# Retention scores of two heads alternating on two halves of the rows, output products grouped by array shape

## The chip, the cores and the metric

The kernel runs on one core of one Trainium2 chip. The core has five engines with queues of their own: TensorE (PE, matrix products), VectorE (DVE), ScalarE (ACT), GpSimd (POOL) and SyncE (SP, which issues most transfers). The metric is the time of one execution on the device in microseconds, the median of several runs.

## The reference

Two layers work on a sequence of 16 meta tokens and 512 tokens with 1024 channels. In each layer a projection feeds three mixers side by side: six heads of stick-breaking attention, six heads of retention (64 channels each), and a state-space mixer (S5). Their outputs are concatenated, projected back, and followed by a gated MLP. The change touches retention alone, which works by chunks of 128 positions:

```python
scores = jnp.einsum('bhnid,bhnjd->bhnij', qc, kc) * decay_in[None, :, None]
inner = jnp.einsum('bhnij,bhnje->bhnie', scores, vc.astype(jnp.float32))
...
cross = jnp.einsum('bhid,bhde->bhie', qn, state)
state = state * chunk_decay[None, :, None, None] + jnp.einsum('bhjd,bhje->bhde', kn, vn)
...
o = inner + jnp.moveaxis(cross, 0, 2)
```

So within a chunk the output is the masked scores times the values, and what came before the chunk enters through the state. The kernel has the decay folded into tables by which q and k are multiplied, so that a plain triangular mask is left. Its five chunks are the first 512 positions in four of 128, and a last one of 16.

## The kernel before

Activations lie with channels on the 128 partitions and the 528 positions along the free dimension. Two heads of 64 channels share a tile: head 0 has partitions 0 to 63, head 1 the rest. The large products (projections, output projection, MLP) are made in three parts of reduced fp32 each, recorded as `pj` with the operands `xh`, `xl` or `hi`, `lo` (activations) and `wh`, `wl` (weights). They are emitted by `mm3`, which after each k step calls `tick`.

The mixers are generators ("lanes") that are resumed by `tick` between the products of a projection, so their instructions are woven into TensorE's queue between `pj` products. What is resumed when is decided by a planner: `spend` (line 96) keeps a clock for each engine, `mm` (line 128) charges a product's estimated time to TensorE's clock, and a lane goes on when its last step's estimated end is at most 200 ns ahead of TensorE's clock. A lane that needs PSUM banks takes credits (`banks`, five in all) and gives them back (`freed`). A scheduler of the framework then orders the emitted instructions once more by its own simulation of readiness. On the chip each engine works through its queue in order and waits on semaphores.

`ret_pair` (line 931) is the lane of one pair of heads; three pairs per layer run one after another, six in all. It transposes v and k (`rtp`), makes the chunk states (`kv`, summed into `st`), and then, from line 968: for each head in turn four score products of 128x128 into one bank `ps` and one of 16x16 into a second bank `ps2` (both recorded as `sc`), with 64 rows of the array each; two DVE operations multiply them by the mask `keep` into an SBUF tile `sc`. Then (line 986) for each chunk the two heads' outputs `ro` from `sc` and `rv`, 64 columns of the array each, and for all chunks but the first a product of the full array that adds the state's part (`ro` from `rm` and `st`). ACT copies the result out (`o`), and a head norm (`hps`), a gate and a split follow. All products of `ret_pair` are fp32; the trace holds two records for each, one for each pass.

The attention lanes (`sb_group`, line 815) make `z` from `sq` and `sk` with 64 rows of the array too; the two heads run as two lanes.

Of the kernel before, what the change touches and what calls it, by code (L numbers as in the profile page):

```python
# [8 lines left out]
F32 = mybir.dt.float32  # L9
# [3 lines left out]
ALU = mybir.AluOpType  # L13
PSUM = bass.MemoryType.PSUM

P = 128
NM = 16
# [33 lines left out]
def width(g):  # L51
    return g[-1][3] + g[-1][2] - g[-1][1]
# [36 lines left out]
def hybrid_kernel(ctx, tc, A, out, dbg=None):  # L89
# [6 lines left out]
    def spend(key, ns):  # L96
        t = now[0]
        start = max(busy[key], busy["PE"])
        if t:
            if key != t[3]:  # L100
                t[3], t[4] = key, t[1]
            start = max(start, t[4])
            t[1] = max(t[1], start + ns + HOP)
        busy[key] = start + ns
# [19 lines left out]
    V = Timed(nc.vector, "V", 70, 1.05)  # L124
# [3 lines left out]
    def mm(out, lhsT, rhs, start, stop, more=False):  # L128

        n = out.shape[-1] / 2.4  # L130
        spend("PE", 2 * max(107.0, 2 * n) if rhs.dtype == F32 else max(107.0, n) + 3)
        nc.tensor.matmul(out, lhsT=lhsT, rhs=rhs, start=start, stop=stop, skip_group_check=more)  # L132

    class TE:
# [18 lines left out]
    def nm(s):  # L153
        uid[0] += 1
        return f"{s}_{uid[0]}"

    def tt(s="t"):
        return tp.tile([P, T], F32, tag="t", name=nm(s))

    def bank(s="b"):  # L160
        return mx.tile([P, 512], F32, tag="mx", name=nm(s))
# [10 lines left out]
    def take(what, n):  # L172

        if free[what] < n:
            yield lambda: free[what] >= n
        free[what] -= n

    def banks(n):
        yield from take("bank", n)

    def freed(n, what="bank"):
        free[what] += n
# [34 lines left out]
    def const(shape, dt, name):  # L217
        return cp.tile(shape, dt, tag=name, name=name)
# [9 lines left out]
    for name, g in (("A", G_A), ("B2", G_B2)):  # L228
        n = width(g)
        m = masks[n] = const([P, n], BF16, "mask" + name)  # L230
        G.memset(m, 0.0)
        for j, q0, q1, o0 in g:
            c = slice(o0, o0 + min(q1 - q0, P))
# [6 lines left out]
    keep = const([P, P], F32, "keep")  # L240
# [98 lines left out]
    def open_ps(nt, s="pj"):  # L339
        return [bank(s), bank(s)] if nt == T else [bank(s)]  # L340
# [82 lines left out]
    def headnorm(t, gcol):  # L423

        s = tt("hsq")
        SC.activation(s, t, AF.Square)
        yield
        yield from banks(2)
        pss = []
        for i in range(2):  # L430
            ps = bank("hps")
            mm(ps[:, :HALF], lhsT=blk, rhs=s[:, HALF * i:HALF * i + HALF], start=True, stop=True)
            pss.append(ps)
        yield
        for i, ps in enumerate(pss):
            rs_from(ps[:, :HALF], s, HALF * i, HALF)
        rs_exp(s)
        yield
        freed(2)
        V.scalar_tensor_tensor(out=t, in0=t, scalar=cols[:, gcol:gcol + 1], in1=s, op0=ALU.mult, op1=ALU.mult)  # L440
        yield
# [489 lines left out]
    def ret_pair(l, p, q, k, vt, gate, res):  # L931
        v = gp.tile([P, 640], F32, tag="g", name=nm("rv"))
        kt = tt("kt")
        for src, dst in ((vt, v), (k, kt)):
            yield from banks(1)
            ps = bank("rtp")
            for j in range(4):
                TE.transpose(ps[:, P * j:P * j + P], src[:, P * j:P * j + P], ident)
            yield
            SC.copy(out=dst[:, :512], in_=ps)  # L940
            yield
            freed(1)
        yield from banks(1)
        ps = bank("rtp")
        TE.transpose(ps[:NM, :P], vt[:, 512:528], ident)
        yield
        SC.copy(out=v[:NM, 512:640], in_=ps[:NM, :P])
        yield
        freed(1)

        st = tt("st")
        G.memset(st, 0.0)
        yield from banks(1)
        ps = bank("kv")
        for j in range(4):
            mm(ps[:, P * j:P * j + P], lhsT=kt[:, P * j:P * j + P], rhs=v[:, P * j:P * j + P], start=True, stop=True)
        yield
        for hh in range(2):
            r, c = slice(64 * hh, 64 * hh + 64), 64 * hh
            SC.copy(out=st[r, c:c + 64], in_=ps[r, c:c + 64])  # L960
        yield
        for j in range(1, 4):
            for hh in range(2):
                r, c = slice(64 * hh, 64 * hh + 64), P * j + 64 * hh
                V.tensor_tensor(out=st[r, c:c + 64], in0=st[r, c - P:c - P + 64], in1=ps[r, c:c + 64], op=ALU.add)
        yield
        freed(1)
        scs = []
        for hh in range(2):
            r = slice(64 * hh, 64 * hh + 64)  # L970
            sc = tt("sc")
            yield from banks(2)
            ps, ps2 = bank("sc"), bank("sc")
            for j in range(4):
                mm(ps[:, P * j:P * j + P], lhsT=k[r, P * j:P * j + P], rhs=q[r, P * j:P * j + P], start=True, stop=True)
            mm(ps2[:NM, :NM], lhsT=k[r, 512:528], rhs=q[r, 512:528], start=True, stop=True)
            yield
            V.tensor_tensor(out=sc[:, :512].rearrange("p (j c) -> p j c", c=P), in0=ps.rearrange("p (j c) -> p j c", c=P),
                            in1=keep[:, None, :].to_broadcast([P, 4, P]), op=ALU.mult)
            V.tensor_tensor(out=sc[:NM, 512:528], in0=ps2[:NM, :NM], in1=keep[:NM, :NM], op=ALU.mult)  # L980
            scs.append(sc)
            yield
            freed(2)
        yield from banks(2)
        op, op2 = bank("ro"), bank("ro")
        for j in range(5):
            n = P if j < 4 else NM
            d = op[:, P * j:P * j + n] if j < 4 else op2[:, :n]
            for hh in range(2):
                r = slice(64 * hh, 64 * hh + 64)  # L990
                mm(d[r], lhsT=v[:n, P * j + 64 * hh:P * j + 64 * hh + 64], rhs=scs[hh][:n, P * j:P * j + n],
                   start=True, stop=j == 0)
            if j:
                mm(d, lhsT=st[:, P * (j - 1):P * j], rhs=q[:, P * j:P * j + n], start=False, stop=True)
            if j == 2:
                yield
        o = tt("o")
        SC.copy(out=o[:, :512], in_=op)
        SC.copy(out=o[:, 512:528], in_=op2[:, :NM])
        yield  # L1000
        freed(2)
        yield from headnorm(o, 80 + 3 * l + p)
        yield lambda: gate() is not None
        rg = gate()
        s = tt("sg")
        V.tensor_scalar(out=s, in0=rg, scalar1=-40.0, scalar2=None, op0=ALU.max)
        yield
        sigmoid(s, s, 1.0)
        yield
        G.tensor_tensor(out=s, in0=s, in1=rg, op=ALU.mult)  # L1010
        yield
        V.tensor_tensor(out=o, in0=o, in1=s, op=ALU.mult)
        dump(f"ro{l}{p}", o)
        yield
        res.append(o)
# [38 lines left out]
    for l in range(LAYERS):  # L1054
# [76 lines left out]
        for ks in OUT_PARTS[l]:  # L1131
            drain(lambda: all(mix[k] is not None for k in ks))
            for m in range(KD):
# [3 lines left out]
                ps = open_ps(nt)  # L1137
# [13 lines left out]
        for n, (kind, i, f0, nf) in enumerate(mlp_order()):  # L1151
            w = weight()
            ps = open_ps(nt)
# [119 lines left out]
```

## Time and profile before

| | us |
|---|---|
| median of three runs | 1395.85 |
| lowest and highest run | 1392.8, 1401.91 |
| profiled execution | 1399.35 |
| its span, first to last instruction | 1397.6 |
| TensorE busy in it | 1370.0 |
| DVE, ACT, POOL busy in it | 807.1, 618.9, 509.2 |

The profile shows one execution. A row of the timeline view is a merged run of like instructions of one engine: its start, its length, the engine, line and operation, the tiles (output, then inputs), the shape (rows*columns of the array that a product uses, then the operands), and how many records it merges; a bracket gives the engine's idle time before it and who ended that. Matmuls overlap, so a length includes the tail of the last one, and the distance between starts is what a stretch costs. In the list of groups three durations are the least, the middle and the greatest in ns.

### The profile page before, as it was taken

To read this page: it belongs to the slowest core of one execution; us is meant where nothing else is said; L and a number is where in the kernel's file an instruction comes from. 1 tells how busy PE (TensorE), PEld (TensorE's weight loads), DVE (VectorE), ACT (ScalarE), POOL (GpSimd) and SP (SyncE) were. 2 spreads that over 40 slices of the span, in tenths; PEclk is the share of its full clock that TensorE was granted. 3 is DMA by queue.
4 is the path that set the end of the run, shared out by engine and by line. 5 is a ranking of instruction groups with operands and counts; after the bars stand their busy time and mean duration, and the time that the engine had idled before them with its cause. 6 is when DMAs were issued, how large, how long until landed. Compare 5 with 4: busy or idle time off the path is not lost.

```text
span 1397.6 us, 22767 instructions
## 1 busy us (share of the span) xinstructions
PE 1370.0 (98%) x9188; PEld 1254.3 (90%) x9188; DVE 807.1 (58%) x1312; ACT 618.9 (44%) x1002; POOL 509.2 (36%) x624
## 2 busy tenths in 40 slices
PE   6999999999999999999999999999999999999998
PEld 6989898999999999999999999998788888888886
DVE  8875557767455545544566477464585543553453
ACT  5456565545343223322354564874363432442231
POOL 5685536322689302200233544362122210220020
PEclk9999799999999999999999999999999999999999
DMA  4212102313221322222222121122232322223223
GB/s 154 69 65 96 38 21 84 97 46 115 97 76 61 106 91 91 90 93 87 80 91 91 61 93 46 56 68 82 79 106 96 100 92 94 101 91 104 93 77 105
DMA packets 38985, 118.27 MB, mean 85 GB/s; under 512 B 4960, under 2 KB 5472, under 8 KB 38880
## 3 DMA queue, kind: packets, MB, share of 16 engines
q1 hardware_dynamic: 38880, 116.82, 25.8%
q8 instruction: 72, 1.18, 0.3%
q14 instruction: 33, 0.27, 0.1%
HBM read 111.46 MB, written 2.10 MB: 81 GB/s over the span
## 4 chain that ended last, share of the span: by engine, by line
PE 85%; DVE 8%; POOL 4%; issue 1%; DMA 1%; ACT 1%; SPq 0%; DVEq 0%; POOLq 0%; ACTq 0%
PE pj L132 71%; PE z L132 6%; PE hps L132 1%; PE ro L132 1%; PE av L132 1%; DVE s5w L121 1%; PE sc L132 1%; PE yps L132 1%; DVE wl L121 1%; POOL lo L121 1%; PE kps L132 1%; DVE sq L121 1%; DVE gg L121 1%; DVE fr L121 0%; PE kv L132 0%
## 5 line engine op out<-in xcount | busy, mean ns | idle before, releaser
L132 PE MATMUL pj<-xh,wh 128*128 128x264 f32 (+1 forms) x1792 | 451.5, 311 | 13.7 <-ACT wh L121 5.2
L132 PE MATMUL pj<-xh,wl 128*128 128x264 f32 (+1 forms) x1792 | 451.6, 311 | 1.6 <-DVE wl L121 1.6
L132 PE MATMUL pj<-xl,wh 128*128 128x264 f32 (+1 forms) x1792 | 449.7, 310 | 1.7 <-DVE xl L121 1.7
L121 ACT CAST wh<-wr 128x1024 fp32r<-128x1024 f32 (+3 forms) x209 | 206.0, 987 | 417.5 <-PE pj L132 381.8
L132 PEld LDWEIGHTS pj<-xh,wh 128*128 128x128 f32 x1792 | 298.3, 191 | 31.3 <-issue 7.5
L132 PEld LDWEIGHTS pj<-xl,wh 128*128 128x128 f32 x1792 | 298.5, 190 | 19.6 <-DVE xl L121 2.4
L132 PEld LDWEIGHTS pj<-xh,wl 128*128 128x128 f32 x1792 | 298.2, 190 | 19.3 <-issue 2.0
L121 DVE TENSOR_TENSOR wl<-wr,wh 128x1024 fp32r<-128x1024 f32 (+3 forms) x166 | 249.2, 1502 | 73.7 <-ACT wh L121 71.3
L132 PE MATMUL pj<-hi,wh 128*128 128x264 f32 (+1 forms) x720 | 192.9, 323 | 0.0
L132 PE MATMUL pj<-lo,wh 128*128 128x264 f32 (+1 forms) x720 | 192.3, 321 | 0.0
L132 PE MATMUL pj<-hi,wl 128*128 128x264 f32 (+1 forms) x720 | 191.7, 321 | 0.1
L121 POOL TENSOR_TENSOR up<-ga,up 128x528 f32<-128x528 f32 (+1 forms) x44 | 61.8, 1405 | 345.6 <-DVE up L121 345.6
L121 DVE TENSOR_TENSOR h<-h,pj 128x264 f32<-128x264 f32 (+1 forms) x144 | 69.2, 511 | 135.1 <-PE pj L132 135.0
L121 POOL TENSOR_TENSOR wl<-wr,wh 128x1024 fp32r<-128x1024 f32 (+2 forms) x43 | 95.6, 2223 | 130.4 <-ACT wh L121 122.9
L132 PEld LDWEIGHTS pj<-hi,wh 128*128 128x128 f32 x720 | 119.4, 188 | 11.0 <-ACT wh L121 0.6
L132 PEld LDWEIGHTS pj<-hi,wl 128*128 128x128 f32 x720 | 119.4, 188 | 10.9 <-DVE wl L121 0.5
L132 PEld LDWEIGHTS pj<-lo,wh 128*128 128x128 f32 x720 | 119.4, 188 | 10.3
L121 POOL TENSOR_TENSOR lo<-ga,hi 128x528 fp32r<-128x528 f32 (+1 forms) x44 | 58.9, 1339 | 158.7 <-ACT hi L121 158.6
L121 DVE TENSOR_TENSOR up<-pj,R 128x264 f32<-128x264 f32 (+1 forms) x66 | 32.2, 515 | 95.2 <-PE pj L132 95.2
L121 ACT ACTIVATE si<-si,bias 128x528 f32<-128x528 f32 (+1 forms) x44 | 32.1, 731 | 94.3 <-DVE si L121 94.3
L121 DVE TENSOR_TENSOR ga<-si,up 128x528 f32<-128x528 f32 (+1 forms) x44 | 31.7, 720 | 72.7 <-ACT si L121 56.8
L121 ACT ACTIVATE e<-z 128x512 f32<-128x512 f32 (+2 forms) x72 | 39.3, 546 | 63.2 <-PE z L132 57.2
(228 smaller groups left out, 1747.1 us busy)
## 6 DMA issues: line engine op xcount, KB each, us to landing
wr<-in_w_in_dram SPq DMA_DIRECT2D x45, 512.0 KB, 3.5
wr<-in_w_gate_dram SPq DMA_DIRECT2D x44, 512.0 KB, 3.4
wr<-in_w_up_dram SPq DMA_DIRECT2D x44, 512.0 KB, 3.4
wr<-in_w_down_dram SPq DMA_DIRECT2D x32, 512.0 KB, 3.4
wr<-in_w_out_dram SPq DMA_DIRECT2D x16, 384.0 KB, 3.2
wr<-in_w_down_dram SPq DMA_DIRECT2D x16, 384.0 KB, 3.1
rc<-in_rope_dram SPq DMA_DIRECT2D x12, 264.0 KB, 3.7
rs<-in_rope_dram SPq DMA_DIRECT2D x12, 264.0 KB, 4.0
```

What stands on the lines that cost most here:

```text
L121: return f(*a, **k)
L132: nc.tensor.matmul(out, lhsT=lhsT, rhs=rhs, start=start, stop=stop, skip_group_check=more)
```

## The change

Three things change. `mm` charges TensorE's clock only half for each product with a 64 among the partitions of its moving operand or output; this holds for the scores, for the outputs from `sc`, and for `z` from `sq`. In the scores, one bank for each head and a shared one for the two 16x16 products are taken together; the 16x16 product of head 0 comes first, then the 128x128 products alternate between the heads, so between rows 0 to 63 and 64 to 127 of the array; the 16x16 product of head 1 follows once DVE has read that of head 0 from the shared bank. In the outputs, all products from `sc` come first, and those from the state after them.

```diff
@@ -128,7 +128,8 @@
     def mm(out, lhsT, rhs, start, stop, more=False):
 
         n = out.shape[-1] / 2.4
-        spend("PE", 2 * max(107.0, 2 * n) if rhs.dtype == F32 else max(107.0, n) + 3)
+        t = 2 * max(107.0, 2 * n) if rhs.dtype == F32 else max(107.0, n) + 3
+        spend("PE", t / 2 if 64 in (rhs.shape[0], out.shape[0]) else t)
         nc.tensor.matmul(out, lhsT=lhsT, rhs=rhs, start=start, stop=stop, skip_group_check=more)
 
     class TE:
@@ -965,35 +966,43 @@
                 V.tensor_tensor(out=st[r, c:c + 64], in0=st[r, c - P:c - P + 64], in1=ps[r, c:c + 64], op=ALU.add)
         yield
         freed(1)
-        scs = []
-        for hh in range(2):
-            r = slice(64 * hh, 64 * hh + 64)
-            sc = tt("sc")
-            yield from banks(2)
-            ps, ps2 = bank("sc"), bank("sc")
-            for j in range(4):
-                mm(ps[:, P * j:P * j + P], lhsT=k[r, P * j:P * j + P], rhs=q[r, P * j:P * j + P], start=True, stop=True)
-            mm(ps2[:NM, :NM], lhsT=k[r, 512:528], rhs=q[r, 512:528], start=True, stop=True)
-            yield
+
+        scs = [tt("sc"), tt("sc")]
+        yield from banks(3)
+        pss, ps2 = [bank("sc"), bank("sc")], bank("sc")
+
+        def score(hh, j):
+            r, n = slice(64 * hh, 64 * hh + 64), P if j < 4 else NM
+            c = slice(P * j, P * j + n)
+            mm(pss[hh][:, c] if j < 4 else ps2[:n, :n], lhsT=k[r, c], rhs=q[r, c], start=True, stop=True)
+
+        def kept_last(sc):
+            V.tensor_tensor(out=sc[:NM, 512:528], in0=ps2[:NM, :NM], in1=keep[:NM, :NM], op=ALU.mult)
+        score(0, 4)
+        for j in range(4):
+            for hh in range(2):
+                score(hh, j)
+        yield
+        kept_last(scs[0])
+        for sc, ps in zip(scs, pss):
             V.tensor_tensor(out=sc[:, :512].rearrange("p (j c) -> p j c", c=P), in0=ps.rearrange("p (j c) -> p j c", c=P),
                             in1=keep[:, None, :].to_broadcast([P, 4, P]), op=ALU.mult)
-            V.tensor_tensor(out=sc[:NM, 512:528], in0=ps2[:NM, :NM], in1=keep[:NM, :NM], op=ALU.mult)
-            scs.append(sc)
-            yield
-            freed(2)
+        score(1, 4)
+        yield
+        kept_last(scs[1])
+        yield
+        freed(3)
         yield from banks(2)
         op, op2 = bank("ro"), bank("ro")
-        for j in range(5):
-            n = P if j < 4 else NM
-            d = op[:, P * j:P * j + n] if j < 4 else op2[:, :n]
+
+        tiles = [(j, P if j < 4 else NM, op[:, P * j:P * j + P] if j < 4 else op2[:, :NM]) for j in range(5)]
+        for j, n, d in tiles:
             for hh in range(2):
-                r = slice(64 * hh, 64 * hh + 64)
-                mm(d[r], lhsT=v[:n, P * j + 64 * hh:P * j + 64 * hh + 64], rhs=scs[hh][:n, P * j:P * j + n],
-                   start=True, stop=j == 0)
-            if j:
-                mm(d, lhsT=st[:, P * (j - 1):P * j], rhs=q[:, P * j:P * j + n], start=False, stop=True)
-            if j == 2:
-                yield
+                mm(d[64 * hh:64 * hh + 64], lhsT=v[:n, P * j + 64 * hh:P * j + 64 * hh + 64],
+                   rhs=scs[hh][:n, P * j:P * j + n], start=j in (0, 4), stop=True, more=True)
+        yield
+        for j, n, d in tiles[1:]:
+            mm(d, lhsT=st[:, P * (j - 1):P * j], rhs=q[:, P * j:P * j + n], start=False, stop=True, more=True)
         o = tt("o")
         SC.copy(out=o[:, :512], in_=op)
         SC.copy(out=o[:, 512:528], in_=op2[:, :NM])
```

All six pairs change alike; the places below are in the program's last pair (second layer) and in the lanes of the first layer. `order` here means the sequence of instructions in one engine's queue, without times.

TensorE, the scores of the last pair before; `rm` are q and k, `pj` are products of the output projection, and x4 merges four like rows:

```order
L132 MATMUL pj_11476<-hi_10871,wh_11395 128x512
L132 MATMUL sc_11483<-rm_11131,rm_11300 128x128 x4
L132 MATMUL sc_11484<-rm_11131,rm_11300 16x16
L132 MATMUL pj_11476<-lo_10872,wh_11395 128x512
L132 MATMUL pj_11476<-hi_10871,wl_11396 128x512
L132 MATMUL pj_11497<-hi_9633,wh_11430 128x512
L132 MATMUL pj_11497<-lo_9634,wh_11430 128x512
L132 MATMUL pj_11497<-hi_9633,wl_11431 128x512
L132 MATMUL sc_11502<-rm_11131,rm_11300 128x128 x4
L132 MATMUL sc_11503<-rm_11131,rm_11300 16x16
L132 MATMUL pj_11497<-hi_10725,wh_11430 128x512
```

There are two stretches of `sc`, one for each head, with `pj` between them.

The same place after the change, from the third of the four alternations on (ahead of these rows stand `sc_11444` 16x16, then twice `sc_11442` and `sc_11443`):

```order
L133 MATMUL sc_11442<-rm_11113,rm_11256 128x128
L133 MATMUL sc_11443<-rm_11113,rm_11256 128x128
L133 MATMUL sc_11442<-rm_11113,rm_11256 128x128
L133 MATMUL sc_11443<-rm_11113,rm_11256 128x128
L133 MATMUL pj_11438<-lo_10816,wh_11375 128x512
L133 MATMUL pj_11438<-hi_10815,wl_11376 128x512
L133 MATMUL pj_11438<-hi_10910,wh_11375 128x512
L133 MATMUL pj_11438<-lo_10911,wh_11375 128x512
L133 MATMUL pj_11438<-hi_10910,wl_11376 128x512
L133 MATMUL sc_11444<-rm_11113,rm_11256 16x16
```

The heads alternate in one stretch, and the second 16x16 product stands alone, five `pj` later.

TensorE, the outputs of the last pair before, from where head 1 joins:

```order
L132 MATMUL ro_11519<-sc_11501,rv_11409 64x128
L132 MATMUL ro_11519<-sc_11482,rv_11409 64x128
L132 MATMUL ro_11519<-sc_11501,rv_11409 64x128
L132 MATMUL ro_11519<-rm_11131,st_11453 128x128
L132 MATMUL ro_11519<-sc_11482,rv_11409 64x128
L132 MATMUL ro_11519<-sc_11501,rv_11409 64x128
L132 MATMUL ro_11519<-rm_11131,st_11453 128x128
L132 MATMUL ro_11519<-sc_11482,rv_11409 64x128
L132 MATMUL ro_11519<-sc_11501,rv_11409 64x128
L132 MATMUL ro_11519<-rm_11131,st_11453 128x128
L132 MATMUL ro_11520<-sc_11501,rv_11409 64x16
L132 MATMUL ro_11520<-rm_11131,st_11453 128x16
```

Products with 64 output rows and products from the state alternate chunk by chunk.

The same place after the change:

```order
L133 MATMUL ro_11465<-sc_11441,rv_11368 64x128
L133 MATMUL ro_11465<-sc_11440,rv_11368 64x128
L133 MATMUL ro_11465<-sc_11441,rv_11368 64x128
L133 MATMUL ro_11465<-sc_11440,rv_11368 64x128
L133 MATMUL ro_11465<-sc_11441,rv_11368 64x128
L133 MATMUL ro_11465<-sc_11440,rv_11368 64x128
L133 MATMUL ro_11465<-sc_11441,rv_11368 64x128
L133 MATMUL ro_11466<-sc_11441,rv_11368 64x16
L133 MATMUL ro_11465<-rm_11113,st_11410 128x128 x3
L133 MATMUL ro_11466<-rm_11113,st_11410 128x16
```

Seven products from `sc` stand together, then the narrow one, then those from the state.

DVE, the masks of the last pair's scores before (`h` are residual additions, `wl` a split of weights), and after:

```order
L121 TENSOR_TENSOR st_11453<-st_11453,kv_11455 64x64 x6
L121 TENSOR_TENSOR sc_11482<-sc_11483,keep 128x512
L121 TENSOR_TENSOR sc_11482<-sc_11484,keep 16x16
L121 TENSOR_TENSOR h_142<-h_142,pj_11476 128x512
L121 TENSOR_TENSOR wl_11513<-wr_11448,wh_11512 128x768
L121 TENSOR_TENSOR sc_11501<-sc_11502,keep 128x512
L121 TENSOR_TENSOR sc_11501<-sc_11503,keep 16x16
```

```order
L121 TENSOR_TENSOR st_11410<-st_11410,kv_11412 64x64 x6
L121 TENSOR_TENSOR h_138<-h_138,pj_11422 128x512
L121 TENSOR_TENSOR sc_11440<-sc_11444,keep 16x16
L121 TENSOR_TENSOR wl_11460<-wr_11396,wh_11459 128x768
L121 TENSOR_TENSOR sc_11440<-sc_11442,keep 128x512
L121 TENSOR_TENSOR sc_11441<-sc_11443,keep 128x512
L121 TENSOR_TENSOR h_139<-h_139,pj_11438 128x512
```

Before, head 0's two masks stand together and head 1's two rows later; after, head 0's small mask comes first, a split of weights stands behind it, and then both large ones.

## Rows read from the trace of the kernel before

**Rows 1.** Page, parts 1 and 4: busy time of engines; the chain by engine

```profile
PE 1370.0 (98%) x9188; PEld 1254.3 (90%) x9188; DVE 807.1 (58%) x1312; ACT 618.9 (44%) x1002; POOL 509.2 (36%) x624
PE 85%; DVE 8%; POOL 4%; issue 1%; DMA 1%; ACT 1%; SPq 0%; DVEq 0%; POOLq 0%; ACTq 0%
```

**Rows 2.** Waits of TensorE: total us, times, longest

```profile
PE pj L132 <- ACT wh L121: 5.2, 1, 5.2
...
PE z L132 <- POOL lo L121: 1.2, 2, 0.6
PE vps L138 <- DVE rg L121: 1.1, 1, 1.1
```

**Rows 3.** Groups of instructions on the tiles `sc` and `ro`, all six pairs

```profile
L132 PE MATMUL sc<-rm,rm x120: 172/272/374, 182.9 to 988.6; 64*128 64x128 f32 x96, 64*16 64x16 f32 x24
...
L132 PE MATMUL ro<-sc,rv x120: 204/273/324, 194.2 to 995.8; 128*64 128x128 f32 x96, 16*64 16x16 f32 x24
...
L132 PE MATMUL ro<-rm,st x48: 262/279/377, 195.6 to 996.0; 128*128 128x128 f32 x36, 128*128 128x16 f32 x12
```

**Rows 4.** Timeline of TensorE, scores of one head in the third pair

```profile
291.28 0.40 PE L132 MATMUL pj<-hi,wh 128*128 128x264 f32 x2
291.53 0.40 PE L132 MATMUL pj<-lo,wh 128*128 128x264 f32 x2
291.86 1.29 PE L132 MATMUL sc<-rm,rm 64*128 64x128 f32 x10
293.09 0.51 PE L132 MATMUL pj<-hi,wl 128*128 128x264 f32 x2
293.43 0.40 PE L132 MATMUL pj<-hi,wh 128*128 128x264 f32 x2
```

**Rows 5.** Timeline of TensorE, a 16-column score that stands alone

```profile
191.03 0.40 PE L132 MATMUL pj<-xl,wh 128*128 128x264 f32 x2
191.37 0.21 PE L132 MATMUL sc<-rm,rm 64*16 64x16 f32 x2
191.51 0.51 PE L132 MATMUL pj<-xh,wl 128*128 128x264 f32 x2
```

**Rows 6.** Timeline of TensorE, outputs of the last pair

```profile
993.12 0.65 PE L132 MATMUL ro<-sc,rv 128*64 128x128 f32 x6
993.70 0.49 PE L132 MATMUL ro<-rm,st 128*128 128x128 f32 x2
994.12 0.44 PE L132 MATMUL ro<-sc,rv 128*64 128x128 f32 x4
994.49 0.49 PE L132 MATMUL ro<-rm,st 128*128 128x128 f32 x2
```

**Rows 7.** Timeline cut at 993.13 us: what had started (PEld: weight loads)

```profile
993.12 0.14 PEld L132 LDWEIGHTS ro<-sc,rv 128*64 128x64 f32 x2 [0.36 <-issue]
993.12 0.33 PE L132 MATMUL ro<-sc,rv 128*64 128x128 f32 x2
```

**Rows 8.** Timeline: scores on TensorE and their masks on DVE, first three pairs

```profile
182.95 1.30 PE L132 MATMUL sc<-rm,rm 64*128 64x128 f32 x10
...
186.34 0.76 DVE L121 TENSOR_TENSOR sc<-sc,keep 128x512 f32<-128x512 f32 x2
...
254.85 1.30 PE L132 MATMUL sc<-rm,rm 64*128 64x128 f32 x10
...
260.00 0.76 DVE L121 TENSOR_TENSOR sc<-sc,keep 128x512 f32<-128x512 f32 x2
...
293.05 0.76 DVE L121 TENSOR_TENSOR sc<-sc,keep 128x512 f32<-128x512 f32 x2 [0.25 <-PE sc L132]
```

**Rows 9.** Busy us by stretch (PE to POOL), granted clock, DMA; then TensorE's timeline

```profile
150.00:158.50 8.50, 7.36 (x55) 6.61 (x53) 8.50 (x10) 4.14 (x10) 8.50 (x6) 1.00 0.21 65
158.70:175.60 16.90, 16.90 (x69) 15.04 (x69) 3.54 (x10) 8.69 (x20) 6.74 (x7) 0.50 0.10 31
...
156.46 0.33 PE L138 MATMUL vps<-ident,sv 128*128 128x128 f32 x1 [1.13 <-DVE rg L121]
```

## The prediction

> **What bounds the kernel now.** I read the page first: TensorE is busy 1370.0 of 1397.6 us, and 85% of the chain that ended last is TensorE [rows 1]. The list of waits then says where it is not busy: one wait of 5.2 us for the first weights, and short ones in the lanes of the first layer, 1.1 before a transpose and 1.2 before `z` products [rows 2]. Everywhere else TensorE is the queue that the others wait for, so a microsecond of its work that goes is a microsecond of the span, as long as no new wait takes its place. The retention part is small in it: 120 records of `sc`, 120 of `ro` from `sc`, 48 of `ro` from the state [rows 3]; an fp32 product is two records (two passes), so these are 60 + 60 + 24 products over six pairs of heads. That is about 2.8 us of scores and 4 us of outputs per pair, and bounds what the change can touch to some 40 us, 3% of the span.
>
> **How the stretches are priced.** The reader should look at starts, not durations, since matmuls overlap. In [rows 4] two full-array `pj` records take 0.24 us from start to start; the two ahead of `sc` take 0.33, so leaving the shape costs 0.09; `sc` takes 1.23 from its start to that of the next `pj`; and that `pj` pair takes 0.34, so entering the new shape costs 0.10 again. One `sc` stretch therefore costs 1.23 + 0.09 + 0.10 = 1.42 us, of which the eight passes of 128 columns are about 0.90, at the 0.11 us for a pass that [rows 6] give below; the rest are two narrow passes and changes of shape. A lone 16-column product costs 0.34, 0.14 from its start to the next `pj` and the same 0.10 on either side [rows 5]. In the outputs the shapes alternate: `ro` from the state takes 0.42 for two passes, `ro` from `sc` 0.37 for two products [rows 6]. With 0.109 per pass (0.58 for the six records that hold three products, 0.37 for the four that hold two: two passes more cost 0.21), both contain 0.22 of passes, so 0.20 + 0.15 = 0.35 us per round trip is change of shape alone.
>
> **Halves of the array.** In the outputs the two heads already write two halves of the columns, and there two products start together: within 0.13 us of the first start two records and two weight loads are under way [rows 7], and the four records of a pair of products cost two passes. For halves of the rows the trace has nothing: the two heads' scores stand in separate stretches, and `z` of the two heads never follow one another directly. The gain of alternating is thus bounded by 0 (one after the other) and by 0.90 per pair (eight passes of 16 hidden). I take 0.90, because the nearest row, the column halves, shows both the streams and the weight loads side by side.
>
> The Trainium skill, page TensorE: Matmul & The Clock Gate, section LDWEIGHTS (loading the stationary operand), says that the time of a load goes by its columns and not by its rows. The trace agrees: `sc` loads 64 rows, and its eight wide passes still fill about 0.9 of the 1.23 us [rows 4]. By that rule, if the loads of the two halves also went one at a time, 16 loads of 0.11 would fill the stretch whatever the streams do, and the sum below would be 4.1 us instead of 9.5; that is the first rival.
>
> **Scores.** Before: two stretches per pair, 2 x 1.42 = 2.84. After, by the order: one stretch of a 16-column product and eight of 128 columns, then, behind other work, a lone 16-column product. With the halves overlapped eight products cost what four do now, so the long stretch is 1.42 again, plus up to 0.10 since the wide product now enters behind the narrow one (0.05 taken): 1.47 + 0.34 = 1.81. Saved: 1.03 per pair, 6.2 us for six; the first pair has a third stretch before, 0.1 more: 6.3.
>
> **Outputs.** In the order, stretches of the 64-column shape fall from 23 to 12 and stretches of `ro` from the state from 24 to 9; the 16-row product still stands alone. Eleven round trips less at 0.35 = 3.9 us. Against that the first product of head 0 now always runs ahead alone, and in the fourth and the first pair that costs one unpaired round more each (0.22): 3.4 us net.
>
> **Planner.** `mm` now charges half for every product with a 64 in it, so `z` too, and every lane shifts a little against the projections. The order has 27 stretches of `z` from `sq` where there were 30; three at 0.28 to 0.38 (two changes, by [rows 4, 5]): 1.0 us. The lanes of the first layer end some 24 to 30 `pj` records later in the program (about 3 us). I cost this at nothing: behind the last `ro` of that layer there are still over 60 `pj` records, some 8 us at 0.122, before the output projection that reads it. If the rest of that lane took longer than these, the excess would be a wait of TensorE.
>
> **The new wait.** The second 16-column score writes the bank that DVE must first have read for head 0; TensorE is in order, so everything behind it waits as well, projections included. Cover is the time from the first 16-column score to the second: eight products (1.0) and, by the order, 5 to 17 `pj` (0.6 to 2.1): 1.7 to 3.2 us, 2.0 in the first pair. DVE answers late in places: in the first pair `sc` ended at 184.25 and DVE began at 186.34, 2.1 us later; in the second 256.15 and 260.00, 3.85 later; in the third DVE itself waited for TensorE [rows 8]. With 0.2 for the small DVE operation itself, the same lags cost 0.3 in the first pair and 0.9 in the second, nothing in the others: 1.2 us. Bounds: 0, and the largest lag everywhere (rival below).
>
> **Sum.** 6.3 + 3.4 + 1.0 - 1.2 = 9.5 us. The profiled execution took 1399.35 us (span 1397.6); it lies 3.5 above the median of the three runs, 1395.85. So 1389.9 against the profiled one, and 1395.85 - 9.5 = 1386 against the median, which I predict.
>
> **Rivals.**
> 1. Row halves do not overlap. Then 0.90 x 6 = 5.4 is lost from the sum: 4.1 left, 1392 us. For it: no row shows such halves. Against: the column halves [rows 7].
> 2. The half-clock stretch goes. From 158.6 to 175.6 us TensorE was granted 0.50 of its clock, 1.2 in place of 2.4 GHz, and was busy all 16.90 us of it; before the fall it had waited 1.13 us for DVE's `rg` and then run narrow `z` products [rows 9]. At full clock that work takes half, so up to 8.5 us hang on this. In the new order that transpose stands 62 rows behind the last product of the `pj` that `rg` empties, where it was 27; 35 rows at some 0.1 us are 3 us of cover, more than the 1.13. So the wait should go. Against: `yps` now stands ahead of the transpose, and what it needs from POOL is late in the trace, so a wait of the same size may come there. Without the stretch: 1386 - 8.5 = 1378.
> 3. Waits, ending about where it began or slower. If DVE answers 3.85 us late at all six second 16-column scores, against the shortest cover of 1.7, each waits 3.85 + 0.2 - 1.7 = 2.35, 14.1 in all: 1395.85 - 10.7 + 14.1 = 1399. It decides from a mean wait of 1.8 us each (10.7 / 6). For it: the first two pairs [rows 8]. Against: the third, where DVE stood ready.
> 4. Each change of half costs a change of shape. Seven changes per pair at 0.19 (0.09 + 0.10) with no overlap: 6 x (0.90 + 1.33) = 13.4 dearer than my sum, 1400 us, slower than before by 3.9. Against: the column halves change without it [rows 7].
>
> The Trainium skill, page TensorEngine Tiling (Array Packing), section PSUM Bottleneck, warns that tiling makes TensorE faster but not the emptying of PSUM. Here that would be rival 3; the lags of [rows 8] agree in two of the three pairs shown.
>
> **How the numbers follow.** My forecast 0.45 (own range 1380 to 1392), rival 1 0.12, rival 2 0.27, rival 3 0.10, rival 4 0.06. The three runs before lie 9 us apart, so about 1%, 14 us, is what a measurement can tell. Faster by over 1% means under 1381.9: rival 2 and a tail of 0.10 of the forecast, 0.37. Slower by over 1% means over 1409.8: the far end of rivals 3 and 4, 0.05. The rest, 0.58, is within 1%. The range goes from a little below rival 2 (1375) to rivals 3 and 4 (1400).
>
> **What the profile will show.** Right: `sc` records of 128 columns starting in twos, a long `sc` stretch of about 1.2 to 1.3 us in place of two; one `ro` stretch of seven products of about 1.0 us; `ro` from the state in one stretch of about 0.9; TensorE's busy time down by about 10 us. Wrong: `sc` records 0.11 apart one by one (rival 1) or 0.3 apart (rival 4); a line "PE sc <- DVE sc" of many microseconds in the waits (rival 3); a granted clock of 1.00 all through the first layer's lanes (rival 2). What I can't see from here is whether the shifted order makes waits elsewhere in the lanes.

## The result and the profile after

The changed kernel takes 1379.17 us (median of 4 runs, 1378.15 to 1384.1), the kernel before 1394.32 beside it: 15.2 us less; the ratio is 0.9893 with a 95% interval of 0.9863 to 0.9923. A second measurement of the same pair gave 0.9895 (0.9876 to 0.9914). That is 7 us below the 1386 forecast, next to the 1378 of rival 2, and inside the range of 1375 to 1400.

The profiled execution took 1384.1 us, its span 1382.4. First its page: busy time of the engines, and the chain of work that ended last, by engine.

```profile
PE 1352.0 (98%) x9188; PEld 1241.3 (90%) x9188; DVE 806.3 (58%) x1312; ACT 618.1 (45%) x1002; POOL 514.6 (37%) x624
PE 75%; DVE 4%; POOL 3%; issue 1%; ACT 1%; SPq 0%; DMA 0%; DVEq 0%; ACTq 0%
```

TensorE is busy 18.0 us less than in [rows 1], and the span is 15.2 shorter; it is still the bound. Its waits (total us, times, longest), where they differ from [rows 2]:

```profile
PE ro L133 <- DVE sc L121: 1.6, 1, 1.6
PE hps L133 <- ACT hsq L121: 1.6, 2, 1.3
...
PE av L133 <- POOL lo L121: 1.3, 1, 1.3
...
PE sc L133 <- DVE sc L121: 0.2, 1, 0.2
```

The waits of [rows 2] before `vps` (for `rg`) and `z` (for `lo`) are gone; others have come, none of them at the second 16x16 score but 0.2 us. The timeline of TensorE in the first pair (start and length in us, instructions, xcount) answers to [rows 4 to 6]:

```profile
178.88 0.21 PE L133 MATMUL sc<-rm,rm 64*16 64x16 f32 x2
179.03 0.51 PE L133 MATMUL pj<-xl,wh 128*128 128x264 f32 x2
...
180.08 1.31 PE L133 MATMUL sc<-rm,rm 64*128 64x128 f32 x18
181.32 0.36 PE L133 MATMUL z<-maskA,identb 128*128 128x432 bf16 x1
...
184.65 0.65 PE L133 MATMUL ro<-sc,rv 128*64 128x128 f32 x4
185.22 0.51 PE L133 MATMUL pj<-xh,wh 128*128 128x264 f32 x2
185.66 1.30 PE L133 MATMUL ro<-sc,rv 128*64 128x128 f32 x16
186.90 0.40 PE L133 MATMUL av<-hi,v 128*128 128x272 f32 x1
...
187.62 1.04 PE L133 MATMUL ro<-rm,st 128*128 128x128 f32 x8
188.51 0.48 PE L133 MATMUL z<-hi,tri 128*128 128x512 f32 x1
```

Eighteen `sc` records, both heads, take 1.24 us from their start to that of `z`; in [rows 4] ten records of one head took 1.23. The same timeline cut at 180.1 us, TensorE's weight loads and its products:

```profile
180.08 0.20 PEld L133 LDWEIGHTS sc<-rm,rm 64*128 64x128 f32 x2
180.08 0.39 PE L133 MATMUL sc<-rm,rm 64*128 64x128 f32 x2
```

The two heads' records start 13 ns apart (180.079 and 180.092) and their loads 14 ns apart; after the first two the pairs follow every 0.112 us. The halves of the rows overlap, streams and loads, as the halves of the columns do in [rows 7]. The stretches of the timeline that answer to [rows 9] (stretch, its length, TensorE's busy time and instructions, granted clock, DMA share, GB/s):

```profile
150.00:158.50 8.50, 8.50 (x68) 1.00 0.20 64
158.50:176.00 17.50, 17.50 (x135) 1.00 0.09 31
```

There is neither the wait nor the half clock behind it. Up to TensorE's last product 13.6 us lie at 0.50, where the kernel before had 27.3.

### The profile page after: what moved, and what is told of

Same layout as the page of the kernel before. It is cut to its first block, busy times and chain, and to the rows that moved or that the text cites. A ratio compares the mean times of both kernels' runs of the same rounds, so it can differ in the third digit from the quotient of the medians.

```text
span 1382.4 us, 22757 instructions
## 1 busy us (share of the span) xinstructions
PE 1352.0 (98%) x9188; PEld 1241.3 (90%) x9188; DVE 806.3 (58%) x1312; ACT 618.1 (45%) x1002; POOL 514.6 (37%) x624
## 3 DMA queue, kind: packets, MB, share of 16 engines
q1 hardware_dynamic: 38880, 116.82, 25.9%
## 4 chain that ended last, share of the span: by engine, by line
PE 75%; DVE 4%; POOL 3%; issue 1%; ACT 1%; SPq 0%; DMA 0%; DVEq 0%; ACTq 0%
PE pj L133 67%; PE z L133 4%; PE ro L133 1%; PE hps L133 1%; PE av L133 1%; PE yps L133 1%; DVE wl L121 1%; DVE y L121 0%; DVE fr L121 0%; POOL st L121 0%; POOL py L121 0%; PE sc L133 0%; POOL gx L121 0%; POOL bb L121 0%; PE rtp L139 0%
## 5 line engine op out<-in xcount | busy, mean ns | idle before, releaser
L133 PE MATMUL pj<-xh,wh 128*128 128x264 f32 (+1 forms) x1792 | 447.8, 310 | 14.6 <-ACT wh L121 5.3
L133 PEld LDWEIGHTS pj<-xh,wl 128*128 128x128 f32 x1792 | 297.0, 191 | 18.7 <-DVE wl L121 1.8
L121 POOL TENSOR_TENSOR lo<-sp,hi 128x432 fp32r<-128x432 f32 (+2 forms) x36 | 46.4, 1301 | 34.4 <-ACT hi L121 34.3
```

What stands on the lines that cost most here:

```text
L121: return f(*a, **k)
```

## The experiments

"`sc` and `ro`" below is, for each record of these tiles, the time from its start to that of TensorE's next record, waits taken off, summed over the 288 records; "waits" is TensorE's idle time in the profiled execution after its first record, of which 7 to 9 us lie in the first 50 us of every kernel; "clock" is the mean granted clock of all runs; "wait at `rg`" says whether TensorE waits the 1.1 us for DVE's `rg` between 155 and 160 us. "Price" is the halved charge in `mm`.

| kernel | us | ratio to before, interval | sc and ro | waits | clock | wait at rg |
|---|---|---|---|---|---|---|
| before | 1394 to 1397 | 1 | 35.6 | 18.8 | 0.992 | yes |
| changed | 1379.2 | 0.9893 (0.9863, 0.9923) | 25.1 | 21.4 | 0.996 | no |
| changed, again | 1382.0 | 0.9895 (0.9876, 0.9914) | 25.1 | 18.7 | 0.995 | no |
| heads in turn | 1381.7 | 0.9895 (0.9863, 0.9926) | 28.4 | 20.0 | 0.996 | no |
| scores only | 1398.3 | 1.0002 (0.9977, 1.0026) | 29.8 | 25.2 | 0.991 | yes |
| outputs only | 1409.0 | 1.0081 (1.0054, 1.0108) | 30.6 | 25.9 | 0.987 | yes |
| price only | 1397.0 | 1.0003 (0.9986, 1.0020) | 35.3 | 21.1 | 0.994 | no |
| no price | 1391.6 | 0.9946 (0.9924, 0.9968) | 25.3 | 22.4 | 0.991 | yes |
| price not for z | 1392.0 | 0.9962 (0.9937, 0.9987) | 25.0 | 22.2 | 0.991 | yes |
| price not for z, `rg` first | 1386.2 | 0.9915 (0.9902, 0.9928) | 25.0 | 20.9 | 0.995 | no |
| four banks | 1380.2 | 0.9867 (0.9845, 0.9888) | 22.8 | 20.9 | 0.994 | no |
| four banks, again | 1379.6 | 0.9873 (0.9860, 0.9886) | 24.4 | 21.0 | 0.994 | no |
| before, transpose later | 1397.3 | 1.0007 (0.9984, 1.0030) | 35.5 | 18.4 | 0.991 | moved |
| before, `rg` first | 1392.2 | 0.9965 (0.9952, 0.9978) | 35.6 | 17.1 | 0.995 | no |

**Scores only.** The kernel before with the scores of the change alone, old outputs, old price.

```diff
-            ps, ps2 = bank("sc"), bank("sc")
+        pss, ps2 = [bank("sc"), bank("sc")], bank("sc")
...
+        for j in range(4):
+            for hh in range(2):
+                score(hh, j)
```

> The kernel before with the new scores alone (alternating halves, shared narrow bank); planner and outputs as before. Theory: the stretches of sc (sum of distances between starts) fall from 14.7 us to about 8.4, ro stays near 21.8, and the time falls by 4 to 7 us against the kernel before, by some 6 more if the half-clock stretch of the first layer's lanes does not come either. Rival (the planner's shift of all lanes made the gain): sc falls the same, but the time stays within 2 us of the kernel before.

`sc` fell from 14.7 to 9.0 us, not quite to the 8.4 expected, and the time stayed. Its waits, three that [rows 2] do not have in this size:

```profile
PE hps L132 <- ACT hsq L121: 3.0, 3, 1.0
...
PE z L132 <- ACT hi L121: 1.7, 2, 1.3
PE rtp L138 <- DVE rm L121: 1.4, 1, 1.4
```

TensorE meets other results unfinished: 6.4 us more waits in this execution against 5.8 saved in `sc` and `ro`. Only 4.2 of the 6.4 can be the edit's. The other 2.2 lie in the first 50 us, where TensorE's order is still that of before; the changed kernel's two executions differ there by 0.9 as well.

This kernel also prices the half clock. Up to its first score, at 175.2 us, TensorE's order is that of before, it waits as long before `vps`, and in this execution the clock stayed up. Its stretch in the columns of the stretches above:

```profile
158.70:175.60 16.90, 16.90 (x132) 1.00 0.10 32
```

Its timeline of TensorE at `vps` and at a later projection record, and then that same record in the timeline of before:

```profile
156.58 0.33 PE L138 MATMUL vps<-ident,sv 128*128 128x128 f32 x1 [1.16 <-DVE rg L121]
...
169.48 0.28 PE L132 MATMUL pj<-xl,wh 128*128 128x264 f32 x1
```

```profile
177.22 0.28 PE L132 MATMUL pj<-xl,wh 128*128 128x264 f32 x1
```

From `vps` to that record it takes 12.90 us here and 20.76 (177.22 - 156.46) before. The stretch of 17.1 us at half clock thus costs TensorE 7.9 us, 0.46 for each.

**Outputs only.** The kernel before with the new order of the outputs alone.

```diff
-            if j:
-                mm(d, lhsT=st[:, P * (j - 1):P * j], rhs=q[:, P * j:P * j + n], start=False, stop=True)
...
+        for j, n, d in tiles[1:]:
+            mm(d, lhsT=st[:, P * (j - 1):P * j], rhs=q[:, P * j:P * j + n], start=False, stop=True, more=True)
```

> The kernel before with the new order of the outputs alone. Theory: sc stays near 14.7 us, ro falls from 21.8 to about 18.1, the time falls by 3 to 5 us where the granted clock is as before. Rival (planner's shift): time within 2 us of the kernel before.

`ro` fell by 5.2 us, and the kernel is the slowest of all. Two rows of its waits:

```profile
PE hps L132 <- ACT hsq L121: 4.1, 3, 1.7
...
PE z L132 <- DVE sk L121: 2.0, 1, 2.0
```

The second of them in TensorE's timeline, and the stretch that follows:

```profile
907.15 1.53 PE L132 MATMUL z<-sq,sk 64*128 64x272 f32 x6 [2.01 <-DVE sk L121]
```

```profile
907.70:921.40 13.70, 13.70 (x49) 0.50 0.27 92
```

A wait of 2.0 us in the second layer, then 13.7 us at half clock that the kernel before does not have; 7.1 us more waits in all, 5.1 of them behind the first 50 us.

**Price only.** `mm`'s half charge alone.

```diff
-        spend("PE", 2 * max(107.0, 2 * n) if rhs.dtype == F32 else max(107.0, n) + 3)
+        t = 2 * max(107.0, 2 * n) if rhs.dtype == F32 else max(107.0, n) + 3
+        spend("PE", t / 2 if 64 in (rhs.shape[0], out.shape[0]) else t)
```

> The kernel before with the halved price in the planner alone; every product as before. Theory: sc and ro stay at 14.7 and 21.8 us; the time moves only by waits and by the time at half clock, between 3 us slower and 7 us faster, and goes with the mean granted clock (0.99 for the profiled run before, 0.995 for the one after). Rival: 8 us or more faster, since the shift of the lanes was the cause.

Nothing measurable in the time, though the mean clock rose from 0.992 to 0.994. The wait at `rg` went, others came (1.9 us before `sc` for `ysm`, 1.8 before `av` for `lo`). No part alone brings anything; the gain is that of the three together.

**Heads in turn.** The changed kernel with the four products of head 0, then the four of head 1; the rest of TensorE's order is the same but for some `ro` and `pj` records that stand a few places off.

```diff
-        for j in range(4):
-            for hh in range(2):
+        for hh in range(2):
+            for j in range(4):
```

> The changed kernel, but in the one score stretch all four wide products of head 0 come first and then all four of head 1, so only the order of these eight differs. Theory (the halves must alternate to overlap): all but one of the four rounds that overlap are lost, sc rises from 8.4 us to 13 or 14, and the time is about 4.5 to 5.5 us above that of the changed kernel, a ratio to the kernel before near 0.993. Rival (one stretch in place of two is what counts, or the engine overlaps both heads whatever their order): sc stays near 8.4 us and the ratio near 0.989.

```profile
179.16 1.85 PE L133 MATMUL sc<-rm,rm 64*128 64x128 f32 x18
180.94 0.36 PE L133 MATMUL z<-maskA,identb 128*128 128x432 bf16 x1
```

The stretch takes 1.78 us in place of 1.24, `sc` 11.5 in place of 8.3. On TensorE alternating is worth 3.2 us, not the 5.4 that no overlap at all would cost: head 1's first record starts at 179.715, 6 ns after head 0's fifth, while head 0's last starts at 180.044. If the queue holds the products as the kernel emits them, TensorE itself pulled the other half of the rows some records forward; no view here shows the queue, and the framework's scheduler may have done it.

The time does not show the 3.2 us. The theory wanted a ratio near 0.993, and 0.9895 is that of the changed kernel (0.9893 and 0.9895), as the rival had it. The intervals reach some 3 to 4 us to either side, and the profiled execution has 1.4 us fewer waits than the changed kernel's first and less time at half clock; so what alternating is worth in the whole kernel stays open.

**No price, and price not for z.** The changed kernel with the old charge for all products, and with the half charge for scores and outputs only.

```diff
-        t = 2 * max(107.0, 2 * n) if rhs.dtype == F32 else max(107.0, n) + 3
-        spend("PE", t / 2 if 64 in (rhs.shape[0], out.shape[0]) else t)
+        spend("PE", 2 * max(107.0, 2 * n) if rhs.dtype == F32 else max(107.0, n) + 3)
```

```diff
-        spend("PE", t / 2 if 64 in (rhs.shape[0], out.shape[0]) else t)
+        spend("PE", t / 2 if half else t)
...
+            mm(pss[hh][:, c] if j < 4 else ps2[:n, :n], lhsT=k[r, c], rhs=q[r, c], start=True, stop=True, half=True)
...
+                   rhs=scs[hh][:n, P * j:P * j + n], start=j in (0, 4), stop=True, more=True, half=True)
```

> Both parts of the change (scores and outputs) with the old price in `mm`, so the lanes advance as before against the projections. Theory: the shorter change of shapes is worth about 10 us whatever the price (sc about 8.4 to 9 us from start to start, ro about 17 to 18), and which waits of TensorE and half-clock stretches come with it is decided by where the lanes happen to fall; so the time lies under the kernel before by 5 to 12 us once the runs are put at equal mean clock. Rival: the halved price is what keeps TensorE from waiting, and without it the waits eat the gain as they did where the scores or the outputs were changed alone; then 1393 us or more and an idle sum of TensorE of 30 us, not 26.

> The changed kernel, but `mm` charges half for the scores and the outputs alone, and the full price for z. Theory: the price of z decides nothing by itself, the time is within 3 us of the changed kernel (a ratio to the kernel before of about 0.99). Rival: it was the halved price of z that shifted the lanes to where the waits before vps and z vanished; then a ratio of 0.996 or more and these waits of about 1.1 to 1.2 us back in the list.

`sc` and `ro` keep their gain in both, 25.3 and 25.0, but only 4 to 8 of the 15 us are left. In the second the rival holds: the price for z matters, since without it TensorE again waits for `rg`, in the timeline of TensorE and the stretch behind it:

```profile
156.04 0.33 PE L139 MATMUL vps<-ident,sv 128*128 128x128 f32 x1 [1.12 <-DVE rg L121]
```

```profile
158.10:175.10 17.00, 17.00 (x70) 0.50 0.10 31
```

The first decides little. By its ratio (7.5 us less) it lies inside the wide range that the theory gave it, and it is only 1.4 us under the rival's bound. Counted as the expectation did, with the 5.3 us before the first record, its waits are 27.5 us, between the theory's 26 and the rival's 30. The halved price is not needed to keep the gain of `sc` and `ro`; without it this kernel too waits 1.1 us before `vps`, though its clock stayed up behind that in the profiled execution.

**Before, transpose later.** The third v's second transpose is held back in the planner.

```diff
+        third = vcalls[0] == 3
         for j0, nj in ((0, 4), (4, 1)):
+            if third and nj == 1:
+                now[0][1] += 1500
+                yield
```

> The kernel before, with one edit: the lane that makes the third v pauses ahead of its second transpose, so that this stands about 100 rows later in TensorE's order and DVE's rg is long done. Theory: the wait of 1.1 us before vps goes, and the half-clock stretch of 17 us that began 2 us behind it goes with it; the mean granted clock rises from 0.991 to 0.994 or more, the time at half clock falls from 23 to about 12 us, and the time falls by 3 to 4 us (17 us at the 0.34 us per us that the runs of the kernel before show is at most 5.8). Prediction's price: 8.5 us. Rival: the stretch comes from the narrow products and not from the wait; the clock stays at 0.991 and the time is the same within 1 us.

TensorE's timeline, and the stretch behind it:

```profile
155.67 0.34 PE L132 MATMUL z<-maskA,identb 128*128 128x432 bf16 x1 [1.12 <-DVE rg L121]
```

```profile
156.90:174.00 17.10, 17.10 (x70) 0.50 0.10 31
```

The wait was not removed but handed on: the next product, a `z`, waits for the same `rg`. The half-clock stretch came forward with it, from 158.6 to 156.9. Clock and time are those of before. The edit did not do what it was for, and decides nothing but that the wait hangs on DVE's `rg` and not on the transpose.

**Before, `rg` first.** So what makes DVE late was moved: one operation `lo` that stood ahead of `rg` goes 36 DVE instructions back (counted in the trace; the expectation says 18).

```diff
-        (lo_eng or V).tensor_tensor(out=R_(b[:, :n]), in0=src[:, :n], in1=a[:, :n], op=ALU.subtract)
+        if late is not None:
+            spend("V", 70 + 1.05 * n)
+            late.append(lambda: nc.vector.tensor_tensor(out=R_(b[:, :n]), in0=src[:, :n], in1=a[:, :n], op=ALU.subtract))
...
+            if len(late) == 3:
+                late.pop(1)()
```

It is charged where it was and issued behind later evictions of projections.

> The kernel before, with one DVE operation of 1.57 us (`lo` from `sbo`, which stood right ahead of the two that empty `rg`'s banks) put 18 DVE instructions later; the order on the other engines is that of before but for four projection rows on TensorE. In the trace of before DVE began the first `rg` at 155.98 and TensorE waited from 155.33 to 156.46 for it; without `lo` ahead DVE begins it at 154.5 and both banks are free by 155.3, so this wait goes whole and is not passed on to the next product, as it was with the later transpose. Theory: the half-clock stretch follows that wait. Then the stretch of 17 us at 158 is absent, the mean granted clock of the runs is 0.994 or more where before has 0.991, and the time falls by the wait, 1.1 us, and by some 11 us less at half clock at 0.34 to 0.46 us each, 3.7 to 5.1: 4.8 to 6.2 us in all, a ratio of 0.9956 to 0.9966. Rival: the stretch has another cause (the narrow products behind the transpose); then the clock stays at 0.991 and at most the 1.1 us of the wait are gained, 0.999.

Its timeline (DVE and TensorE), then the stretches:

```profile
152.72 0.76 DVE L121 TENSOR_TENSOR rg<-pj,R 128x264 f32<-128x264 f32 x2
...
153.38 0.33 PE L138 MATMUL vps<-ident,sv 128*128 128x128 f32 x1
```

```profile
150.00:158.50 8.50, 8.38 (x64) 1.00 0.38 124
158.70:175.60 16.90, 16.90 (x125) 1.00 0.00 1
```

No wait there, no half clock, and 1392.2 us beside 1396.6: 4.4 less (by the ratio, 3.1 to 6.7), where the theory expected 4.8 to 6.2 and the rival at most 1.1. The mean clock of the runs is 0.995 beside 0.991. One DVE operation of before, moved, gives a third of what the whole change gives.

**Price not for z, `rg` first.** The same move in the changed kernel with full price for z.

> The changed kernel with the full price for z, and the same DVE operation moved behind `rg`. Theory: most of what the halved price of z gave the changed kernel was that the wait before vps, and the half-clock stretch behind it, went; so without that wait this kernel comes close to the changed one: clock 0.994 or more where it was 0.991, and 4.8 to 6.2 us less than the 1392.0 us without the move, 1386 to 1387. Rival: the halved price gave its gain otherwise (fewer changes of shape, fewer waits later on): no more than 1 to 2 us less, 1390 us or more.

1386.2 as expected, a ratio of 0.9915 after 0.9962: some two thirds of what the price of z is worth (0.9962 against 0.9893) is the wait at `rg` and its half clock. For the last 3 to 4 us, down to the changed kernel's 1382.0 on this chip, the intervals of the two ratios overlap; they stay open.

**Changed kernel again, and four banks.** The changed kernel unaltered, on the chip of the last two runs; and with a bank for each of the two 16x16 scores, so that all ten scores of a pair stand together and none waits for DVE.

```diff
-        pss, ps2 = [bank("sc"), bank("sc")], bank("sc")
+        pss, ps2s = [bank("sc"), bank("sc")], [bank("sc"), bank("sc")]
...
         score(0, 4)
+        score(1, 4)
```

> The changed kernel with a bank of its own for each of the two 16x16 scores, so that all ten scores of a pair are one stretch and the second 16x16 score waits for nothing. Theory: no line PE sc <- DVE sc in the waits, one change of shape and back less per pair (about 0.3 us by the lone 16-column product), sc about 7 us from start to start where the changed kernel has 8.4, and 1 to 3 us less time. Rival: four banks come free later than three, the lane begins its scores later and DVE's masks and the outputs with it; then new waits of TensorE of 1 us and more before ro or av and no gain or a loss.

> The changed kernel as it is, beside the others on the same chip, as the measure for them, with a second profile of it. Expected: a ratio to the kernel before of 0.986 to 0.992, a mean clock of 0.995 to 0.997; no stretch of half clock at 158, since there is no wait there; the sums of sc (8.4) and ro (18.1) from start to start as in the first profile within 0.3 us.

> The kernel with a bank for each of the two 16x16 scores, beside the changed kernel on the same chip. Theory: it is faster than the changed kernel by what its shorter stretches save, sc 1.0 and ro 2.7 us less from start to start, less about 0.3 to 0.5 us for more time at half clock: 2 to 3 us, about 1377. Rival: the new waits (1.7 us before ro, 1.9 us for ysm) eat that: within 1 us of the changed kernel or slower.

Two rows of the first run with four banks (first pair), and its wait in the fourth pair:

```profile
180.23 1.31 PE L133 MATMUL sc<-rm,rm 64*16 64x16 f32 x20
184.84 1.67 PE L133 MATMUL ro<-sc,rv 128*64 128x128 f32 x20
...
838.04 1.69 PE L133 MATMUL ro<-sc,rv 128*64 128x128 f32 x20 [1.70 <-DVE sc L121]
```

`sc` 7.4, one stretch in each pair, and `ro` 15.4; in the second execution `ro` took 17.0, since in the fourth pair it ran 3.4 us at half clock behind the same wait of 1.70. The rival's new wait before `ro` is there, but it comes from DVE's `y` running late, as in the changed kernel (last section), not from the fourth bank. The time is 1379.6 beside 1382.0 for the changed kernel on the same chip: as expected in size (2.4 us), but the intervals of the two ratios overlap, so it is likely and not shown that this version is faster. It has the lowest ratio of all kernels on both its chips.

## Why the prediction was right, and where not

**Scores and outputs: right.** Predicted 6.3 and 3.4. `sc` fell from 14.7 to 8.3 us, 6.4, and `ro` from 20.9 to 16.8, 4.0 without waits and 3.7 with them. The row halves overlap, which rivals 1 and 4 denied. The Trainium skill, page TensorE: Matmul & The Clock Gate, section LDWEIGHTS (loading the stationary operand), gives a load's time by its columns. Rival 1 took the loads of the two halves as going one at a time; the trace shows them side by side, 0.18 us each and 14 ns apart.

**z: too large.** Predicted 1.0. With the records at half clock counted at 0.54 of their time (by the 0.46 above) the `z` records take 93.1 us before and 92.6 after: 0.5 (0.8 in the second execution).

**The new wait: right in size, wrong in place.** I put 1.2 us at the second 16x16 score of the first two pairs. It costs 0.2 in all, in the fourth pair. What DVE's lag costs instead is 1.6 us before `ro` in the fourth pair, where a large mask comes late, in one of two profiled executions (below).

**Waits elsewhere: the step that failed.** The sum holds all other waits as they were; the end of the prediction says that it cannot see them. They are where much of the parts' gain went when made alone (4.2 and 5.1 us more behind the first 50 us) and where the changed kernel won something: the wait at `rg` went, as rival 2 has it. The fear for `yps` there did not come true. The later end of the first layer's lanes cost nothing, as assumed: between 222 and 365 us TensorE has no wait in either execution. In the profiled executions the sum of TensorE's waits is 2.6 us higher after, in the second one the same.

**Rival 2: right in kind, too dear.** What I took for a rival is part of the result. It was priced at 8.5 us, half of one stretch in one execution. The stretch costs 7.9 on the spot. But the kernel before does not have it in every run: in 58 runs its mean clock lies between 0.988 and 0.998 and the time rises by 0.35 us for each us at half clock (correlation 0.94), less than the 0.46 on the spot; why some of it comes back later stays open. By the mean clocks the changed kernel runs 11 to 12 us less at half clock, worth 4 to 5.5 us. The kernel before with `rg` first, 4.4 us faster, shows this by itself. So the forecast and rival 2 were not two cases: 6.4 + 4.0 + 0.5 + 4 to 5.5, less up to 2.6 for waits, is 12 to 16 us, and 15.2 and 14.6 were measured. In the two profiled executions the account closes: 10.4 for `sc` and `ro`, 0.5 for `z`, 1.4 for all other products, 5.6 for 12.3 us less of TensorE's work at half clock (at the 0.46), less 2.6 for waits, make 15.3, and the spans differ by 15.2.

So the time of 1379.2 does not confirm the 9.5 us of the sum. It lies just outside the forecast's own 1380 to 1392, and the wide range held because it was drawn from rival to rival.

**Does the half clock follow the wait?** In every kernel with the wait for `rg` (moved or not) the mean clock is 0.987 to 0.992, in every kernel without it 0.994 to 0.996, and the one moved DVE operation that takes this wait away brought two kernels from the first group to the second. That is shown. That the wait always brings the stretch is not: scores only, outputs only and no price waited there in the profiled execution and kept their clock behind it. In the two executions with four banks the same wait of 1.70 us before `ro` left the clock up once and was followed by 3.4 us at half clock the other time. What else decides stays open.

## What to carry to other kernels

Where two small products use different halves of the array, put them next to each other in the queue and keep one shape together: the direct gain on TensorE could be read from starts in the trace to within 0.6 us a term (that alternating shows in the whole time is not measured). But in woven lanes a shorter piece moves all that follows, and what each wait and the clock behind it cost was as much as the gain: made alone, two of three parts brought nothing and one lost 0.8%. Before pricing a rearrangement, list the waits near 1 us that it may make or remove, and ask which operation ahead in the late engine's queue could simply go behind.

## What the runs showed of the hardware

**Which of DVE and POOL starts first decides 2.2 us.** The fourth pair of the changed kernel in the timeline (DVE, POOL and TensorE), in the first profiled execution and then in the second:

```profile
835.46 2.38 POOL L121 TENSOR_TENSOR wl<-wr,wh 128x1024 fp32r<-128x1024 f32 x1 [1.36 <-ACT wh L121]
835.47 2.93 DVE L121 TENSOR_TENSOR y<-fi,phi 128x528 f32<-128x528 f32 x1
...
839.05 0.43 PE L133 MATMUL ro<-sc,rv 128*64 128x128 f32 x2 [1.65 <-DVE sc L121]
```

```profile
831.95 0.71 DVE L121 TENSOR_TENSOR y<-fi,phi 128x528 f32<-128x528 f32 x1
831.95 2.96 POOL L121 TENSOR_TENSOR wl<-wr,wh 128x1024 fp32r<-128x1024 f32 x1 [1.37 <-ACT wh L121]
...
833.83 0.43 PE L133 MATMUL ro<-sc,rv 128*64 128x128 f32 x2
```

The same two operations meet. POOL began 10 ns ahead (835.457 and 835.467), and DVE's `y` took 2.93 us; DVE began 1 ns ahead (831.950 and 831.951), and `y` took 0.71 and POOL's `wl` 0.6 more. The first order of start made TensorE wait 1.65 us for the mask behind `y`; the second none. The Trainium skill, page SBUF — State Buffer, section Who interferes with whom, says that a DVE instruction with two SBUF inputs contends with a GpSimd instruction that reads SBUF, and that issue order decides who blocks; the trace agrees: `y` ended 0.56 us after `wl`, so most of it ran behind it. The other kernels' traces agree: where these two meet in the fourth pair, POOL began 46 and 55 ns ahead with four banks, and `y` took 2.89 and 2.88 us; in five kernels DVE began 62 to 139 ns ahead, and `y` took 0.69 to 0.71. The operation that made `rg` late in the kernel before, `lo` with 1.57 us, took 0.69 where it was moved to.

**Two row halves overlap in part when the kernel does not alternate them**: 0.37 us per pair of heads of the 0.9 that alternating hides (heads in turn). Whether TensorE or the scheduler brings this about is not shown.
